# One decoder layer on one core: steps and rates of three mixing streams, and the order of the first products

## Chip, core and metric

The kernel runs on one core of a Trainium2 chip. It is one launch, and the metric is the device time of that launch in microseconds (us). Of the core's engines, TensorE (PE) multiplies and transposes, VectorE (DVE), ScalarE (ACT) and GpSimd (POOL) do the rest, and SyncE (SP) issues most transfers. Each engine works through its own queue in order.

## What is computed

One layer of a decoder: a gated feed-forward network, a mixer of two parts side by side, and a second feed-forward network, each between root-mean-square norms. It is applied to 1,024 prompt tokens and to 8 x 8 tokens of running sequences. All is float32.

```python
x = x + 0.5 * rms_norm(swiglu(rms_norm(x, norm_ffn1_pre), ffn1_w_gu, ffn1_w_down), norm_ffn1_post)
z = rms_norm(x, norm_mix_pre) @ w_in + b_in            # q, k, v, hq, hf, hi, hg
a = rms_norm(window_attention(q, k, v, sinks), attn_out_norm)          # 8 heads of 64, window 128
f = lb + (1 - lb) * sigmoid(hf)
o, S = hgrn2(silu(hq), 1 - f, log(f), hi, s0)                          # 4 heads, state 128 x 128
o = rms_norm(o, hg_out_norm) * silu(hg)
x = x + rms_norm(concat([a, o]) @ w_out, norm_mix_post)
x = x + 0.5 * rms_norm(swiglu(rms_norm(x, norm_ffn2_pre), ffn2_w_gu, ffn2_w_down), norm_ffn2_post)
```

`swiglu(x, w_gu, w_down)` is `(silu(x @ g) * (x @ u)) @ w_down` with g and u the two halves of `w_gu`; the model width is 1,024, the inner width 2,816.

## The kernel before, in words

**Tiling.** The 1,088 tokens form three groups: group 0 has 320 (256 of the prompt and the 64 sample tokens), groups 1 and 2 have 384 each (`WIDTH`, line 26). A float32 product is made of three passes (`mm3`, lines 277 to 281): both factors are split into a rounded high part and the remainder, and high by high, high by low and low by high are added in PSUM. `split` (line 257) makes the two parts, the rounding on ACT (line 258), the subtraction on DVE (line 259). Weights come in tiles of 128 x 1024 (512 KB) through three `raw` buffers, and `Ahead` (line 74) requests and splits two or three of them ahead. PSUM has eight banks, four named `mm` for the wide products and four named `ax` for everything else.

**Streams.** Work that is not a wide product is written as generators, and each `yield` ends a step. `stream(name, gen, rate)` (line 97) starts one. Each `tick()` (line 100) adds the rate to the stream's credit, and a step is traced for every whole credit. `need(name)` (line 110) traces all that is left. Ticks stand between the wide products: in a unit of `up0` (line 684) after every half of a weight tile, that is, after 12 products. So the order of a trace is wide products with steps of the streams between them; a scheduler that simulates the program then lays out each engine's queue from it.

**Mixing.** `mixer(n)` (line 1506) alternates, step by step, a recurrent side (`intra`, line 1230, then `hgrn_block` for every 128 tokens, line 1324) and an attention side (`attn_block`, line 1161); for n = 0 the samples' parts are appended to each. When one side has ended, the other gets all steps. In `intra`, each of seven levels h = 64 ... 1 multiplies parts of K (line 1299) by a decay on POOL, over all blocks at once. Then `hgrn_block` transposes K (kT, line 1335). `attn_block` computes scores (sc, line 1178), exponentials (line 1195), transposes (pT, line 1206) and products with v (pv, line 1219). `finish_attn` (line 1144) and `finish_hgrn` (line 1306) normalise 128 rows, yield once, and transpose them (oT, line 1154; hT, line 1318). The rates of the three mixers are `RM = [0.95, 1.0, 1.3]` (line 1560). Mixer 0 runs under the last products of the first feed-forward network and `w_in_units(1)`, mixer 1 under `w_out_units(0)`, `w_in_units(2)` and five units of the second network's head, mixer 2 under `w_out_units(1)` and nine such units. Other streams run beside them: c0, c1 and c2 (norms between the parts; `pre_s`, line 477, has the large splits of lines 499 and 501).

**Head.** `load_x(0, True)` (line 548) requests x of group 0 in six parts, the first halves of the columns on SP's queue and the second halves on ACT's; then two whole weight tiles follow on SP's. `pre_first` (line 556) begins with 23 products of ones that nobody reads (`warm`, line 564), transposes the gain row, and takes the sums of squares, three on ACT (line 577) and three on DVE (line 578). For each of the eight column blocks d it transposes x (line 598), after d = 1 come seven more products of ones, rounds the two parts of h (lines 605, 606), keeps x (line 607), and multiplies block d - 1 by both weight tiles of the first unit. The norm's factor is not in h yet: its row sum is broadcast by one product (rb, line 619) and multiplied in behind the products, in `both0` (line 697), for the first four units. `scaled` (line 630) makes the scaled h for all later units.

Of the kernel before, what the change touches and what calls it, by code (L numbers as in the profile page):

```python
# [8 lines left out]
F32 = mybir.dt.float32  # L9
# [5 lines left out]
ALU = mybir.AluOpType  # L15
# [24 lines left out]
NRAW = 3  # L40
WARM = 23, 7
P1 = 1.4
# [3 lines left out]
def tile_step(ctx: ExitStack, tc: tile.TileContext, A: dict, O: list):  # L46
# [10 lines left out]
    def uid(s):  # L57
        cnt[0] += 1
        return f"{s}_{cnt[0]}"

    def mmbank():
        return ps.tile([P, 512], F32, tag="mm", bufs=4, name=uid("mm"))

# [74 lines left out]
    def first_gain():  # L138
        rows = cp.tile([KC, P], F32, name="rows1")
        nc.sync.dma_start(rows, A["norm_ffn1_pre"].rearrange("o (c p) -> (o c) p", p=P))  # L140
        return rows
# [405 lines left out]

    def load_x(n, two=False):
        y = [big(F32, (P, 3, 512)), big(F32, (P, 3, 512))]
        for i in range(3):  # L550
            for hf in range(2):
                (nc.scalar if two and hf else nc.sync).dma_start(
                    y[hf][:rows_of(n, i), i], x_rows(n, i)[:, hf * 512:hf * 512 + 512])
        return y

    def pre_first(y, rows, gpre, h, raws, wts, part):

        w = WIDTH[0]  # L560
        sm = small()
        spare = axbank()

        def warm(n):
            for _ in range(n):
                last = PE.matmul(spare[:, :P], ones, ones, start=True, stop=True).ins
            return last

        last_tr = warm(WARM[0])
        V.memset(sm[:, 0, :], 1.0)  # L570
        junk2 = tmp2("junk")
        gt = axbank("gt")
        PE.transpose(gt[:, :KC], rows, ident[:KC, :KC])
        V.tensor_copy(gpre, gt[:, :KC])
        for i in range(3):
            r = rows_of(0, i)
            S.activation(junk[:r], y[0][:r, i], AF.Square, scale=D ** -0.5, accum_out=sm[:r, 0, i:i + 1])
            V.scalar_tensor_tensor(junk2[:r], y[1][:r, i], 1.0 / D, y[1][:r, i], op0=ALU.mult, op1=ALU.mult,
                                   accum_out=sm[:r, 0, 4 + i:5 + i])
        tiles = []  # L580
        for raw in raws:
            hi, lo = [pp.tile([P, KC, P], F32R, tag="wsp", bufs=8, name=uid("w")) for _ in range(2)]
            for ks in (slice(0, 4), slice(4, 8)):
                split(hi[:, ks], lo[:, ks], raw[:, ks])
            tiles.append((hi, lo))
        banks = [mmbank(), mmbank()]
        hx, x = new_h(1), [big(), big()]

        def products(d):
            for wt, bank in zip(tiles, banks):  # L590
                mm3(bank[:, :w], (wt[0][:, d, :], wt[1][:, d, :]), hcol(hx, d, w), d == 0, d == KC - 1)

        for d in range(KC):
            bank = axbank("tr")
            with tc.issue_after(last_tr):
                for i in range(3):
                    r = rows_of(0, i)
                    tr = PE.transpose(bank[:, i * P:i * P + r], y[d // 4][:r, i, (d % 4) * P:(d % 4) * P + P],
                                      ident[:r, :r])
                last_tr = tr.ins  # L600
                if d == 1:
                    last_tr = warm(WARM[1])
            hi, lo = hcol(hx, d, w)
            g = gpre[:, d:d + 1]
            last_hi = S.activation(hi, bank[:, :w], AF.Copy, scale=g)
            V.scalar_tensor_tensor(lo, bank[:, :w], g, hi.bitcast(F32), op0=ALU.mult, op1=ALU.subtract)
            (V.tensor_copy if d % 2 else S.copy)(x[d // 4][:, d % 4, :w], bank[:, :w])
            if d:
                products(d - 1)
            if d == 2:  # L610
                V.scalar_tensor_tensor(sm[:, 0, 0:3], sm[:, 0, 0:3], EPS, sm[:, 0, 4:7], op0=ALU.add, op1=ALU.add)
                rsqrt(sm[:, 1, 0:3], sm[:, 0, 0:3], (sm[:, 2, 0:3], sm[:, 3, 0:3]))
                dg = tmp2("dg")
                for i in range(3):
                    r = rows_of(0, i)
                    V.tensor_scalar(dg[:, i * P:i * P + r], ident[:, :r], sm[:, 1, i:i + 1], None, op0=ALU.mult)
            if d == 4:
                bank = axbank("rb")
                PE.matmul(bank[:, :w], ones, dg[:, :w], start=True, stop=True)
                rb = tmp2("rb")[:, :w]  # L620
                S.copy(rb, bank[:, :w])
            if d == 1:
                with tc.issue_after(last_hi.ins):
                    wts.fill()
        products(KC - 1)
# [10 lines left out]
        return (hx, rb), banks, scaled  # L636

# [11 lines left out]
    def make_ffn(wgu, wdn, h, tag):  # L649
# [33 lines left out]

        def up0(j, wts, act=None):

            w = WIDTH[0]
            g, u = mmbank(), mmbank()
            for bank in (g, u):
# [354 lines left out]
    def mixing(tp, h):  # L1043
# [100 lines left out]
        def finish_attn(n, o, r, sl):  # L1144
# [85 lines left out]
        def intra(n, res):  # L1230
# [37 lines left out]
            for h in reversed(LEVELS):  # L1268
# [11 lines left out]
                else:  # L1280
                    per = 3 if h == 32 else 2
                    for b0 in range(0, NPB[n], per):
# [8 lines left out]
                        for c in range(0, P, 2 * h):  # L1291
# [6 lines left out]
                                op=ALU.mult)  # L1298
                G.tensor_tensor(Kv[:, :, :, :h], Kv[:, :, :, :h], Dv[:, :, :, 1:2].to_broadcast([P, 4, nx, h]),
                                op=ALU.mult)  # L1300
                if h == 4:
# [4 lines left out]
        def finish_hgrn(n, bank, r, c0):  # L1306
# [6 lines left out]
            rsqrt(sm[:r, 1, :4], sm[:r, 0, :4], (sm[:r, 2, :4], sm[:r, 3, :4]))  # L1313
            V.tensor_tensor(o[:r], b4[:r], sm[:r, 1, :4].unsqueeze(2).to_broadcast([r, 4, P]), op=ALU.mult)
            yield
            tb = axbank("hT").rearrange("p (a t) -> p a t", a=4)
# [242 lines left out]

    RM = [0.95, 1.0, 1.3]  # L1560
    RA0, RA1, RB0, RB1 = 1.2, 0.75, 0.6, 0.8
# [9 lines left out]
    rows1 = first_gain()  # L1571
    xs = [load_x(0, True)]
    h = {}
    f1 = make_ffn(A["ffn1_w_gu"][0], A["ffn1_w_down"][0], h, 1)
    w0 = f1.loads0(first[1:])
    part = {}
    act, unit0, scaled = pre_first(xs[0], rows1, f1pre, h, [f1.raw0(c) for c in (first[0] * P, DFF + first[0] * P)], w0, part)
    f1.gated0(first[0], unit0, act[1])
    scaled(range(0, 2))
# [185 lines left out]
```

## Time and profile before

| | |
|---|---|
| median of 3 runs | 1997.62 us (1997.28 to 1998.98) |
| the profiled execution's own time | 1997.85 us |
| its span in the profile | 1996.1 us |
| mean granted TensorE clock | 0.995 |
| DMA | 370.28 MB, 185 GB/s |

The span is the time from the first to the last instruction of one execution. In rows of the timeline the first number is the start in us from the span's start, the second the duration in us of all the instructions in the row, then engine, line, operation, what is written and read, and how many; a bracket holds the engine's idle time just before and what ended it. In rows by stretches each engine has its busy us and its instructions, in the order PE, PEld (loading the stationary operand), DVE, ACT, POOL, then the granted TensorE clock (1.00 is full), the DMA engines' share and GB/s. TensorE's busy time includes the pipelined ends of its products, so rows overlap.

### The profile page before, as it was taken

What the parts mean: (1) busy time and instruction counts of PE and PEld (TensorE: products, weight loads), DVE (VectorE), ACT (ScalarE), POOL (GpSimd) and SP (SyncE); (2) the same over time, 40 slices, a digit from 0 to 9 for tenths busy, and PEclk for the clock granted to TensorE, in tenths of its full rate; (3) what the DMA queues carried; (4) which work ended last, traced back from release to release, by engine and by line L of the source; (5) the groups of instructions that cost most, each with busy time, mean ns of one, the idle gap of its engine ahead of it and who ended that gap; (6) DMA issues with size and microseconds to landing.
All of it is one profiled execution on the core that took longest, in us unless ns stands there. A gap on an engine that the chain in (4) does not pass through costs nothing.

```text
span 1996.1 us, 34286 instructions
## 1 busy us (share of the span) xinstructions
PE 1977.9 (99%) x13331; PEld 1859.0 (93%) x13331; DVE 1405.0 (70%) x2522; ACT 942.3 (47%) x1713; POOL 153.1 (8%) x142
## 2 busy tenths in 40 slices
PE   9999999999999999999999999999999999999998
PEld 9999999999998988779999998989999999999886
DVE  7686767886568656777668656746887887655667
ACT  5753334444445434435344543756544444444452
POOL 0000000000003102210211202000000000000201
PEclk9999999999999999999999999989999999999999
DMA  7735545655777647766334342536565555667874
GB/s 233 221 107 185 189 161 188 227 189 192 234 231 218 183 145 247 233 176 183 108 102 133 95 155 86 171 130 200 165 201 199 191 187 190 211 232 234 287 262 139
DMA packets 377316, 370.28 MB, mean 185 GB/s; under 512 B 40546, under 2 KB 294321, under 8 KB 377137
## 3 DMA queue, kind: packets, MB, share of 16 engines
q1 hardware_dynamic: 371169, 357.21, 56.3%
q10 hardware_dynamic: 5984, 10.88, 1.6%
q8 instruction: 104, 1.70, 0.3%
q14 instruction: 59, 0.48, 0.1%
HBM read 284.31 MB, written 84.71 MB: 185 GB/s over the span
## 4 chain that ended last, share of the span: by engine, by line
PE 96%; DMA 1%; ACT 1%; DVE 1%; issue 0%; POOL 0%; SPq 0%; DVEq 0%; ACTq 0%; POOLq 0%
PE mm L279 28%; PE mm L280 28%; PE mm L281 28%; PE pv L1219 1%; PE sc L1178 1%; PE c L281 1%; PE c L279 1%; PE c L280 1%; DMA raw<-in_ffn_w_gu_dram 1%; PE pT L1206 1%; PE lv L1258 1%; PE tr L511 1%; PE av L1341 0%; PE u L1348 0%; PE av L1344 0%
## 5 line engine op out<-in xcount | busy, mean ns | idle before, releaser
L279 PE MATMUL mm<-h,wsph 128*128 128x320 f32 (+1 forms) x1280 | 406.4, 319 | 0.4 <-ACT sg L676 0.4
L280 PE MATMUL mm<-h,wsph 128*128 128x320 f32 (+1 forms) x1280 | 406.1, 318 | 0.0
L281 PE MATMUL mm<-h,wspl 128*128 128x320 f32 (+1 forms) x1280 | 403.3, 317 | 0.0
L259 DVE TENSOR_TENSOR wspl<-raw,wsph 128x1024 fp32r<-128x1024 f32 x200 | 247.9, 1240 | 151.5 <-ACT wsph L258 145.9
L258 ACT CAST wsph<-raw 128x1024 fp32r<-128x1024 f32 x200 | 209.3, 1048 | 299.1 <-PE mm L280 238.4
L258 ACT CAST w<-raw 128x512 fp32r<-128x512 f32 (+1 forms) x218 | 160.3, 740 | 213.7 <-PE mm L280 113.4
L279 PEld LDWEIGHTS mm<-h,wsph 128*128 128x128 f32 x1280 | 240.7, 188 | 5.5 <-issue 3.8
L259 DVE TENSOR_TENSOR w<-raw,w 128x512 fp32r<-128x512 f32 (+1 forms) x218 | 186.6, 860 | 84.0 <-ACT w L258 83.6
L280 PEld LDWEIGHTS mm<-h,wsph 128*128 128x128 f32 x1280 | 241.0, 188 | 3.1 <-issue 2.7
L281 PEld LDWEIGHTS mm<-h,wspl 128*128 128x128 f32 x1280 | 240.3, 188 | 1.5 <-issue 1.2
L279 PE MATMUL mm<-h,w 128*128 128x384 f32 (+1 forms) x720 | 240.3, 335 | 0.5 <-ACT w L258 0.5
L280 PE MATMUL mm<-h,w 128*128 128x384 f32 (+1 forms) x720 | 240.8, 335 | 0.0
L281 PE MATMUL mm<-h,w 128*128 128x384 f32 (+1 forms) x720 | 235.4, 334 | 0.0
L280 PE MATMUL mm<-w,h 128*128 128x512 f32 x462 | 181.9, 394 | 0.0
L281 PE MATMUL mm<-w,h 128*128 128x512 f32 x462 | 180.3, 392 | 0.0
L279 PE MATMUL mm<-w,h 128*128 128x512 f32 x462 | 180.1, 393 | 0.0
L279 PE MATMUL mm<-big,w 128*128 128x384 f32 x528 | 176.4, 334 | 0.7 <-ACT big L770 0.7
L280 PE MATMUL mm<-big,w 128*128 128x384 f32 x528 | 176.5, 334 | 0.0
L281 PE MATMUL mm<-big,w 128*128 128x384 f32 x528 | 176.2, 334 | 0.0
L279 PEld LDWEIGHTS mm<-h,w 128*128 128x128 f32 x720 | 135.0, 188 | 1.1 <-ACT w L258 0.7
L280 PEld LDWEIGHTS mm<-h,w 128*128 128x128 f32 x720 | 135.2, 188 | 0.1
L281 PEld LDWEIGHTS mm<-h,w 128*128 128x128 f32 x720 | 134.7, 188 | 0.1
(355 smaller groups left out, 3531.3 us busy)
## 6 DMA issues: line engine op xcount, KB each, us to landing
raw<-in_ffn_w_gu_dram SPq DMA_DIRECT2D x156, 512.0 KB
raw<-in_ffn_w_down_dram SPq DMA_DIRECT2D x74, 512.0 KB
raw<-in_w_in_dram SPq DMA_DIRECT2D x54, 512.0 KB
ar<-fa SPq DMA_DIRECT2D x70, 384.0 KB
big<-in_ffn_w_down_dram SPq DMA_DIRECT2D x88, 256.0 KB
fb<-big SPq DMA_DIRECT2D x44, 512.0 KB
fa<-big SPq DMA_DIRECT2D x22, 768.0 KB
raw<-fb SPq DMA_DIRECT2D x30, 512.0 KB
```

Source lines behind the costliest of these rows:

```text
L258: S.copy(hi, src)
L259: (lo_eng or V).tensor_tensor(lo, src, hi.bitcast(F32), op=ALU.subtract)
L279: PE.matmul(out, a[0], b[0], start=first, stop=False, skip_group_check=resume)
L280: PE.matmul(out, a[0], b[1], start=False, stop=False, skip_group_check=resume)
L281: return PE.matmul(out, a[1], b[0], start=False, stop=last, skip_group_check=resume).ins
L511: PE.transpose(bank[:, i * P:(i + 1) * P], y[kh][:, i, k * P:(k + 1) * P], ident)
L1178: PE.matmul(banks[g][:, i * 256:i * 256 + wk], zq[64 * g:64 * g + 64, 2 * pr + i, b * P:(b + 1) * P], kx[64 * g:64 * g + 64, k0:k0 + wk], ...
L1206: PE.transpose(bank[:, (i * nk + kb) * P:(i * nk + kb + 1) * P], pt[g][:, i, kb * P:(kb + 1) * P], ident)
L1219: PE.matmul(ob[:, hd * 64:hd * 64 + 64], pT[g][:, (i * nk + kb) * P:(i * nk + kb + 1) * P], vn[:, vb, g * 64:g * 64 + 64], start=kb == 0, ...
L1258: PE.matmul(b5[32 * i:32 * i + 32, b, a], K[:, a, cs], Q[:, a, cs], start=True, stop=True)
```

## The change

Streams: one more `yield` ahead of the transposes in `finish_attn` and `finish_hgrn`; other rates; POOL's multiplication at level 64 in two instructions, the first block apart.

```diff
@@ finish_attn
             V.tensor_scalar(o[:r], o[:r], sm[:r, 1, 0:1], None, op0=ALU.mult)
+            yield
             yield
             b4 = axbank("oT").rearrange("p (c t) -> p c t", c=4)
@@ intra
-                G.tensor_tensor(Kv[:, :, :, :h], Kv[:, :, :, :h], Dv[:, :, :, 1:2].to_broadcast([P, 4, nx, h]),
-                                op=ALU.mult)
+                for xs in [slice(0, 1), slice(1, nx)] if h == 64 else [slice(0, nx)]:
+                    G.tensor_tensor(Kv[:, :, xs, :h], Kv[:, :, xs, :h],
+                                    Dv[:, :, xs, 1:2].to_broadcast([P, 4, xs.stop - xs.start, h]), op=ALU.mult)
@@ finish_hgrn
             V.tensor_tensor(o[:r], b4[:r], sm[:r, 1, :4].unsqueeze(2).to_broadcast([r, 4, P]), op=ALU.mult)
+            yield
             yield
             tb = axbank("hT").rearrange("p (a t) -> p a t", a=4)
@@
-    RM = [0.95, 1.0, 1.3]
+    RM = [0.85, 0.95, 1.2]
```

Head: twelve products of ones instead of 23 and seven; x and half weight tiles requested in one function, into buffers of the pool `big`, with the half tiles of both weights ahead of x's second column half; all squares on ACT; transposes, roundings and products in an order written out by hand, in which each engine's instruction is issued after the one named before it on that engine; the second unit's products inside the same function; the third unit's sums in `ax` banks.

```diff
-WARM = 23, 7
+WARM = 12
+    def load_first(rows, ws):
+        y = [big(F32, (P, 3, 512)), big(F32, (P, 3, 512))]
+        raws = [big(F32, (P, KC, P)), big(F32, (P, KC, P))]
+        def x_part(q, hf, i):
+            q.dma_start(y[hf][:rows_of(0, i), i], x_rows(0, i)[:, hf * 512:hf * 512 + 512])
+        nc.sync.dma_start(rows, A["norm_ffn1_pre"].rearrange("o (c p) -> (o c) p", p=P))
+        x_part(nc.sync, 0, 0)
+        x_part(nc.scalar, 0, 1)
+        x_part(nc.sync, 0, 2)
+        nc.scalar.dma_start(raws[0][:, 0:4], ws[0][:, 0:4])
+        nc.sync.dma_start(raws[1][:, 0:4], ws[1][:, 0:4])
+        for i in range(3):
+            x_part(nc.sync, 1, i)
+        for raw, w in zip(raws, ws):
+            nc.sync.dma_start(raw[:, 4:8], w[:, 4:8])
+        return [y], raws
@@ pre_first
+        def order(e, made):
+            last[e] = made.ins
+            return made
+        def after(e):
+            return tc.issue_after(last[e]) if e in last else nullcontext()
+        def squares(hf):
+            for i in range(3):
+                r = rows_of(0, i)
+                order("S", S.activation(junk[:r], y[hf][:r, i], AF.Square, scale=D ** -0.5,
+                                        accum_out=sm[:r, 0, 4 * hf + i:4 * hf + i + 1]))
+        def half(n, ks):
+            raw, (hi, lo) = raws[n], tiles[n]
+            with after("S"):
+                order("S", S.copy(hi[:, ks], raw[:, ks]))
+            with after("V"):
+                order("V", V.tensor_tensor(lo[:, ks], raw[:, ks], hi[:, ks].bitcast(F32), op=ALU.subtract))
...
+        for d in range(4):
+            turned(d)
+        squares(0)
+        half(0, lo4)
+        rounded(0)
+        rounded(1)
+        products(0, range(2))
+        half(1, lo4)
+        rounded(2)
+        rounded(3)
+        products(0, range(2, 4))
+        for d in range(4):
+            kept(d)
+        turned(4)
+        turned(5)
+        products(1, range(4))
+        for d in (4, 5):
+            rounded(d)
+        half(0, hi4)
+        turned(6)
+        turned(7)
+        half(1, hi4)
+        for d in (6, 7):
+            rounded(d)
+        products(0, range(4, 8))
+        products(1, range(4, 8))
+        with after("S"), after("V"):
+            wts.fill(1)
+        for d in range(4, 8):
+            kept(d)
+        with after("S"):
+            squares(1)
+        with after("S"), after("V"):
+            wts.fill(2)
+        V.tensor_tensor(sm[:, 0, 0:3], sm[:, 0, 0:3], sm[:, 0, 4:7], op=ALU.add)
...
+        rb = tmp2("rb")[:, :w]
+        second = [mmbank(), mmbank()]
+        for n, bank in enumerate(second):
+            wt = wts.next()
+            for d in range(KC):
+                with after("PE"):
+                    if n and d == 4:
+                        rbank = axbank("rb")
+                        order("PE", PE.matmul(rbank[:, :w], ones, dg[:, :w], start=True, stop=True))
+                        S.copy(rb, rbank[:, :w])
+                    last["PE"] = mm3(bank[:, :w], (wt[0][:, d, :], wt[1][:, d, :]), hcol(hx, d, w), d == 0, d == KC - 1)
...
-        f1.up0(first[1], w0, act)
         scaled(range(2, 5))
-        f1.up0(first[2], w0, act)
+        f1.up0(first[2], w0, act, axbank)
```

`turned(d)` is the transposes of column block d, `rounded(d)` its two parts of h (high on ACT, low on DVE), `kept(d)` the copy of x, and `products(n, ds)` the products of blocks ds with weight tile n, each with the duties it had before.

More of the change, by code (lines that the diff above doesn't have):

```diff
@@ L567, in warm @@
             return last
[L569 to L574, printed above, removed]
+        tiles = [[pp.tile([P, KC, P], F32R, tag="wsp", bufs=8, name=uid("w")) for _ in range(2)] for _ in raws]
+        banks = [mmbank(), mmbank()]
+        hx, x = new_h(1), [big(), big()]
+        last, held = {"PE": warm(WARM)}, {}
+        def order(e, made):
+            last[e] = made.ins
+            return made
@@ new lines, in half, with products @@
+        def half(n, ks):
[4 more added lines that the diff above has]
+                order("V", V.tensor_tensor(lo[:, ks], raw[:, ks], hi[:, ks].bitcast(F32), op=ALU.subtract))
+        def products(n, ds):
+            for d in ds:
+                with after("PE"):
+                    last["PE"] = mm3(banks[n][:, :w], (tiles[n][0][:, d, :], tiles[n][1][:, d, :]), hcol(hx, d, w),
+                                     d == 0, d == KC - 1)
@@ new lines, in kept @@
+        def kept(d):
+            out = x[d // 4][:, d % 4, :w]
+            if d % 2:
+                with after("V"):
+                    order("V", V.tensor_copy(out, held[d][:, :w]))
+            else:
+                with after("S"):
+                    order("S", S.copy(out, held[d][:, :w]))
+        lo4, hi4 = slice(0, 4), slice(4, 8)
+        for d in range(4):
[5 more added lines that the diff above has]
+        products(0, range(2))
@@ L587, in pre_first @@
[L587 to L624, printed above, removed]
```

58 lines of the change are left out of this document (36 added, 22 removed).

## The prediction

> **What bounds the kernel now.** The page came first, then the sums of who waited for whom on TensorE, then stretches of five microseconds wherever the granted clock was below one, then the timeline around the longest waits and of the head.
>
> ```profile
> span 1996.1 us, 34286 instructions
> PE 1977.9 (99%) x13331; PEld 1859.0 (93%) x13331; DVE 1405.0 (70%) x2522; ACT 942.3 (47%) x1713; POOL 153.1 (8%) x142
> ```
>
> TensorE is busy 99% of 1996.1 us. The diff neither adds nor removes a product, so the time can change only where TensorE stands still, or runs at a lower clock, or does work that computes nothing. These are its waits of 0.6 us and more behind the head (columns: us in total, times, longest):
>
> ```profile
> PE pT L1206 <- ACT t L1195: 2.9, 1, 2.9
> PE kT L1335 <- POOL big L1299: 2.4, 1, 2.4
> PE hT L1318 <- DVE t L1314: 0.9, 1, 0.9
> PE tr L468 <- DVE h L473: 0.9, 1, 0.9
> PE mm L279 <- ACT big L770: 0.7, 1, 0.7
> PE skT L1379 <- DMA kv<-in_cache_k_win_dram: 0.6, 1, 0.6
> ```
>
> Some 8.4 us, small. But the clock makes two of them dearer. The column after POOL is the granted clock:
>
> ```profile
> 1230.00:1235.00 5.00, 5.00 (x29) 5.00 (x28) 2.20 (x11) 4.50 (x12) 0.00 (x0) 0.66 0.00 0
> 1295.00:1300.00 5.00, 2.10 (x12) 1.40 (x10) 1.94 (x5) 4.28 (x10) 0.00 (x0) 0.86 0.54 140
> 1300.00:1305.00 5.00, 5.00 (x19) 3.67 (x17) 1.10 (x2) 4.27 (x9) 0.00 (x0) 0.50 0.19 73
> 1305.00:1310.00 5.00, 5.00 (x16) 3.85 (x16) 1.56 (x8) 0.36 (x1) 0.00 (x0) 0.50 0.10 35
> 1310.00:1315.00 5.00, 5.00 (x32) 4.91 (x31) 1.39 (x6) 2.75 (x10) 0.00 (x0) 0.77 0.00 0
> ```
>
> After the 2.4 us wait the clock is short by 0.34 x 5 = 1.7 us. After the 2.9 us wait it is short by 0.14 x 5 + 0.50 x 5 + 0.50 x 5 + 0.23 x 5 = 6.85 us, because what follows there are transposes and narrow attention products, and the clock comes back only in the last of these rows, when the wide products are under way again. The third mixer thus loses 2.4 + 1.7, 0.9 and 2.9 + 6.85: 14.75 us, nearly all that the middle of the kernel has to give.
>
> [...]
>
> **The change part by part: POOL's split (kT).** The rows of the 2.4 us wait:
>
> ```profile
> 1227.41 2.19 POOL L1299 TENSOR_TENSOR big<-big,big 128x768 f32<-128x768 f32 x1 [3.05 <-PE l L1289]
> ...
> 1229.65 0.66 PE L1335 MATMUL kT<-ident,big 128*128 128x128 f32 x4 [2.39 <-POOL big L1299]
> ...
> 1230.34 0.59 ACT L1337 COPY t<-kT 128x512 f32<-128x512 f32 x1 [2.66 <-PE kT L1335]
> ...
> 1233.20 0.61 PE L279 MATMUL mm<-h,wsph 128*128 128x320 f32 x1
> ```
>
> TensorE finishes the 64-level products at 1227.26 (1229.65 less 2.39), POOL scales K in one pass of 2.19 us over three blocks, and kT of block 0 waits for all of it. ScalarE sits in order behind kT's copy, so the banks of the dense products are not emptied either. Split, the first block is one third, 0.73 us; kT starts 1.46 us earlier and the wait is 0.93 us. The wait of 0.9 us at hT, near 1249, left no stretch below a clock of one, so the 1.7 us of clock go too: 3.2 us. The extra POOL instruction lies behind the first slice, on an engine busy 8%, and the next reader of blocks 1 and 2 is a hgrn block later. Bounds: no gain, if the half clock has come from the mixture of work, to 4.1 us.
>
> **The added steps (hT, oT).** The wait of 0.94 us is this:
>
> ```profile
> 1248.20 0.69 DVE L1314 TENSOR_TENSOR t<-av,sm 128x512 f32<-128x512 f32 x1
> ```
>
> The normalisation ends just as its transposes come up. One more yield is about two more ticks, each twelve products, at 0.147 us (13.72, 13.87, 14.01 below) 1.76 us. It covers 0.94 us: minus 0.9. What it costs is one 128 x 512 buffer of eight held for one step more; the PSUM bank is already free by then. Bounds 0 to 0.9.
>
> **The rates (pT).** The rows of the 2.9 us wait (start, duration, engine):
>
> ```profile
> 1287.34 1.22 PE L1178 MATMUL sc<-kx,big 64*128 64x256 f32 x8
> ...
> 1288.31 1.46 ACT L499 CAST h<-big 128x1536 fp32r<-128x1536 f32 x1
> ...
> 1291.92 1.75 DVE L501 TENSOR_TENSOR h<-big,h 128x1536 fp32r<-128x1536 f32 x1
> ...
> 1294.20 0.16 DVE L1189 SCALAR_TENSOR_TENSOR sm<-sm,sinkb 128x4 f32<-128x4 f32 x1
> ...
> 1295.69 1.04 ACT L258 CAST wsph<-raw 128x1024 fp32r<-128x1024 f32 x1 [2.47 <-PE mm L280]
> ...
> 1296.75 1.28 ACT L1195 ACT_TABLE_LOAD   x1
> ...
> 1298.70 2.17 PE L1206 MATMUL pT<-ident,t 128*128 128x128 f32 x8 [2.90 <-ACT t L1195]
> ```
>
> Between scores and exponentials DVE does a 1.75 us subtraction of another stream, c1 (pre_s, line 501); the small maximum row at 1294.20 sits behind it, and then the exponentials sit behind a weight cast and a table load. I count the steps in the code. mixer(2) has 52 steps, its end included; with 3 more at each side 58. Its ticks until need("m2") are 16 in w_out_units(1) and 9 x 4 in the head units: 52. Before, it needs 52 / 1.3 = 40 of them, after, 58 / 1.2 = 48.3. The recurrent side runs out after 40 steps before (tick 31) and 46 after (tick 38), and from then the attention steps stand closest together; that is the place of this wait. The stream c1 has 19 steps at 0.8, so it takes ticks 16 to 40. Before, the tail of the attention (ticks 31 to 40) lies on c1's two large splits; after (38 to 48), almost wholly behind them. Taking 1.75 us off DVE and 1.46 us off ScalarE covers 2.9 us. I take the whole wait and its clock: 9.7 us. Bounds: 0 if the weight cast and the table load alone hold it, 9.75.
>
> All three mixers must end in time: mixer(0) has 74 steps, at 0.85 that is 87 ticks of 24 + 12 + 12 + 44 = 92; mixer(1) 57 at 0.95, 60 of 80. They fit, with 5, 20 and 3.7 ticks left.
>
> **New waits.** Every queue's order is laid out anew. The nearest rows are the two waits in the first mixer's stretch, 0.94 and 0.62 us (tr, skT), and none in the second's. I charge two stages with as much again: plus 3.1 us. Bounds: 0, and 9.75 for one wait like pT.
>
> **The head.** Before, in stretches of 2 us (the first x is TensorE's passes, the last column GB/s), then in order of time:
>
> ```profile
> 0.00:2.00 2.00, 0.88 (x4) 0.88 (x5) 0.46 (x4) 1.20 (x1) 1.20 (x8) 1.00 0.01 2
> 2.00:4.00 2.00, 2.00 (x11) 2.00 (x11) 0.00 (x0) 0.39 (x2) 0.30 (x1) 1.00 0.76 263
> 4.00:6.00 2.00, 2.00 (x16) 2.00 (x15) 0.70 (x2) 0.72 (x2) 0.00 (x0) 1.00 0.99 322
> ```
>
> ```profile
> 1.12 7.23 PE L566 MATMUL ax<-ones 128*128 128x128 f32 x46 [1.12 <-DVE sm L570]
> ...
> 5.27 0.63 ACT L577 ACTIVATE junk<-big 128x512 bf16<-128x512 f32 x1 [2.86 <-DMA big<-in_x_prompt_dram]
> ...
> 10.16 1.14 ACT L258 CAST w<-raw 128x512 fp32r<-128x512 f32 x2 [0.75 <-DMA raw<-in_ffn_w_gu_dram]
> ...
> 10.81 0.69 DVE L259 TENSOR_TENSOR w<-raw,w 128x512 fp32r<-128x512 f32 x1 [0.21 <-ACT w L258]
> ...
> 11.20 0.94 ACT L605 ACTIVATE h<-tr,f1pre 128x320 fp32r<-128x320 f32 x2
> ...
> 12.16 1.00 DVE L606 SCALAR_TENSOR_TENSOR h<-tr,f1pre,h 128x320 fp32r<-128x320 f32 x2
> ...
> 12.95 0.58 PE L598 MATMUL tr<-ident,big 128*128 128x128 f32 x3
> ...
> 13.47 0.42 PE L280 MATMUL mm<-h,w 128*128 128x320 f32 x1
> ...
> 13.72 0.31 PE L281 MATMUL mm<-h,w 128*128 128x320 f32 x1
> ...
> 13.87 0.31 PE L280 MATMUL mm<-h,w 128*128 128x320 f32 x1
> ...
> 14.01 0.31 PE L279 MATMUL mm<-h,w 128*128 128x320 f32 x1
> ```
>
> From 13.47 the products run on without a wait. Four transpose groups (0.52 each, 12.95 to 13.47) and two products are done by then, 2.4 us of useful work, so it is as if it had begun at 11.1. After: x's first half and the half weight tiles are 640 and 512 KB, 1.18 MB; 0.53 MB have come by 4.0 (263 GB/s over two), the rest at 322 GB/s by 6.0, and as the two queues interleave I take 7 for the last of them. ScalarE, in its fixed order: three squares from 5.3 at 0.72 each (0.63 and its accumulator), with the short block's landing about 7.4; half cast 0.57, two roundings 0.47 each, half cast, two roundings: 10.4. DVE follows each with 0.68 or 0.50 and ends the fourth rounding at 11.4. TensorE has transposed by 8 and follows the roundings; after 11.55 it does two transpose groups (1.05), 12 products (1.76), two groups, and 24 products, bar 0.1: about 19. Of these 19 us 8 x 0.52 + 48 x 0.147 = 11.2 are useful: begun at 7.8, 3.3 us earlier. The later half of x, now wholly on SP's queue behind a weight half, lands about 9, needed at 11.55; the upper weight halves by 11, needed at 13.2. The second half's squares, moved from DVE to ScalarE, stand behind the second unit's first weight cast, 2.2 us ahead of a weight that is needed at 22.5. The third unit's sums go to attention banks, which are free, because the first two hold all four others until the row sum is there.
>
> What is late next is DVE:
>
> ```profile
> 28.00:44.00 16.00, 16.00 (x111) 16.00 (x111) 15.41 (x28) 9.41 (x17) 0.00 (x0) 1.00 0.63 186
> ```
>
> While it gated the first units and scaled the second normalisation it was busy 15.41 of 16 us, and TensorE just did not wait. After, the row sum's product stands 36 products behind 19, at about 24.3, where it stood among the transposes, and the same work is due 3.3 us earlier. I take off 1.0: minus 2.3. Bounds: minus 3.3 and plus 2 (the four transpose groups, 2.1 us, at half clock).
>
> A dozen dummy products instead of 23 (46 passes at 1.12) are 24 passes; by the rows of 4, 11 and 16 passes they end at 5.1, just as the pace has doubled. [...]
>
> **The sum.** -3.2 - 0.9 - 9.7 + 3.1 - 2.3 = -13.0 us, from the profiled execution's 1997.85 (span 1996.1 and 1.75 around it): 1984.85. That execution stands 0.23 above the median of 1997.62: 1984.6.
>
> **The rivals.** (a) The pT wait stays, or one of its kind comes back elsewhere: 1984.6 + 9.7 = 1994.3 at most, 1992 with a shorter half clock. For: weight cast and table load stay ahead of the exponentials. Against: the other five pT pairs of the third mixer did not wait. (b) The head gains nothing: a cold clock doubles 2.1 us of transposes and what lies ahead of 11.5, and the fixed order lets one late transfer stop three engines; with +2 instead of -2.3 it is 1988.9. For: it is a row of dependencies with ScalarE in each. Against: TensorE waits there anyway. (c) The streams only shuffle their waits: all of 14.75 lost again, 1997.62 - 2.3 = 1995.3, within 0.2%. That is also the case that the yields do not do what they should, if the order in the queues is not the program's. (d) Slower: the rates are too low. If my count of ticks is off by over 3.7 for mixer(2) and 5 for mixer(0), need() empties the rest with no dense product between. Scores to exponentials without cover is 1287.34 to 1298.70, 11.4 us, of which 7 to 9 bare with the clock halved behind, some 15 us, and once more in mixer(0), where wide products follow sooner, 10: 1984.6 - 3.1 + 25 = 2006.5.
>
> **How the numbers follow.** A measurement of this kernel tells about 0.2% (4 us) from no change. Forecast 0.48 (1978 to 1990), (a) 0.20, (b) 0.11, (c) 0.12, (d) 0.09. Faster by over 0.2%, below 1993.6: 0.48 + 0.11 + three quarters of (a), 0.74 + 0.04 for the better end of (c): 0.78. Within: the rest of (a) and (c), 0.13. Slower: (d), 0.09. Range: the low end takes the head's 3.3 and 3 us fewer new waits, 1980.6, and the waits of the first mixer (1.6) and the gate's whole 0.9 at kT: 1978; the high end takes in (a), (b) and most of (c): 1997.
>
> **What would show it.** POOL's line in two forms at the last level, kT's wait below 1 us; no pT wait and clock 1.00 from 1230 to 1315; no hT wait; first product at about 8.5 and 48 of them done by 19. Wrong, if a stretch at clock 0.50 appears in any mixer, if need() leaves scores and exponentials side by side, or if TensorE waits between 20 and 50 for DVE.

## The result, and the profile after

| | before | after |
|---|---|---|
| median of 4 executions each | 1998.30 us (1997.28 to 1999.31) | 1975.05 us (1974.46 to 1979.19) |
| ratio, 95% interval | | 0.9888 (0.9871 to 0.9905) |
| profiled execution | 1997.85 us, span 1996.1 | 1975.32 us, span 1973.6 |

The kernel is 22.6 us faster than the 1997.62 on which the prediction was made. Forecast were 13.0, and the range ended at 1978.0, 3 us above the result. The direction was right, the size was not, and the sum of steps hides that two of them were wrong in what they stand for.

First the page's head and TensorE's waits after (us in total, times, longest; there are no others):

```profile
span 1973.6 us, 34235 instructions
PE 1960.7 (99%) x13295; PEld 1846.4 (94%) x13295; DVE 1405.5 (71%) x2517; ACT 952.5 (48%) x1724; POOL 153.7 (8%) x145
...
PE ax L278 <- ACT wsph L257: 1.7, 1, 1.7
PE av L1427 <- DVE big L1378: 1.2, 1, 1.2
PE ax L586 <- DVE sm L601: 1.1, 1, 1.1
PE mm L279 <- DVE h L1222: 1.0, 1, 1.0
PE mm L279 <- DVE h L639: 0.3, 1, 0.3
```

Behind the head only two waits are left, 1.2 + 1.0 = 2.2 us; before there were 8.9 us of them. None of before's is here: not pT, not kT, not hT, and not the four small ones either. The stretches behind kT, which now starts at 1221.83, and around the third mixer's last score products, where the clock was at half before (it is the column after POOL):

```profile
1220.00:1225.00 5.00, 3.81 (x43) 3.48 (x42) 3.32 (x3) 1.95 (x4) 1.68 (x2) 1.00 0.51 155
1225.00:1230.00 5.00, 5.00 (x39) 4.98 (x38) 3.52 (x15) 4.95 (x21) 0.00 (x0) 1.00 0.30 112
...
1295.00:1300.00 5.00, 5.00 (x37) 4.99 (x36) 1.88 (x4) 4.19 (x11) 0.00 (x0) 1.00 0.37 108
1300.00:1305.00 5.00, 5.00 (x40) 4.41 (x39) 3.58 (x10) 3.75 (x6) 0.00 (x0) 1.00 0.44 112
1305.00:1310.00 5.00, 5.00 (x38) 4.99 (x36) 2.00 (x9) 4.36 (x11) 0.00 (x0) 1.00 0.37 131
```

Full clock throughout. So far this is what the prediction asked to see, although the pT wait did not go for the reason that it gave (see the rates, below). What it did not look for shows only when TensorE's groups are set side by side, by line and shape (busy us, mean ns of one). Of before:

```profile
L1178 PE MATMUL sc<-kx,big 64*128 64x256 f32 x112 | 25.7, 421 | 0.0
```

and of after:

```profile
L1259 PE MATMUL sc<-kx,big 64*128 64x256 f32 x112 | 18.1, 402 | 0.0
```

The same 112 score products take 7.6 us less, though one of them by itself takes about as long as before. The timeline says why. Before, in the third mixer:

```profile
1238.78 1.13 PE L1178 MATMUL sc<-kx,big 64*128 64x256 f32 x4
...
1242.22 1.13 PE L1178 MATMUL sc<-kx,big 64*128 64x256 f32 x4
```

After, the same products:

```profile
1232.96 1.13 PE L1259 MATMUL sc<-kx,big 64*128 64x256 f32 x8
```

A group of eight works on two head groups, whose operands lie on the first and on the last 64 partitions. Standing next to each other in TensorE's queue, all eight take as long as four of one head group alone: 1.06 us from the first start to the next instruction's, against twice 1.06 when other work lies between. Counted over the whole trace, 7 of the 14 groups were apart before and 2 are after, so 5 x 1.06 = 5.3 us went; the rest of the 7.6 is the half clock of one group near 1305, which the clock's term counts.

The head, in order of time after:

```profile
9.00 0.42 PE L278 MATMUL mm<-h,w 128*128 128x320 f32 x1
...
15.03 3.10 SPq L707 DMA_DIRECT2D xT<-big  x2
...
19.12 0.31 PE L278 MATMUL mm<-h,wsph 128*128 128x320 f32 x1
...
27.71 1.04 ACT L257 CAST wsph<-raw 128x1024 fp32r<-128x1024 f32 x1 [5.96 <-DMA raw<-in_ffn_w_gu_dram]
...
28.81 0.41 PE L278 MATMUL ax<-h,wsph 128*128 128x320 f32 x1 [1.65 <-ACT wsph L257]
```

At 19.12 the first unit's 48 products and all transposes are done, where 19 was forecast; by the forecast's own arithmetic the useful work began at 7.9, 3.2 us earlier than before. But at 28.81 TensorE waits 1.65 us for a weight tile of the third unit, so about 1.5 us are left.

**The account in spans** (1996.1 to 1973.6, 22.5 us): pT's wait and clock 9.75; kT's 4.1, less the new 1.2 at av behind it, 2.9; hT 0.9; the small waits 2.6 less the new 1.0, 1.6; scores 5.3; head 1.5. Together 21.95; 0.55 stay unassigned.

### The profile page after: what moved, and what is told of

It reads as the page before. It is cut to its first block, busy times and chain, and to the rows that moved or that the text cites. A ratio compares the mean times of both kernels' runs of the same rounds, so it can differ in the third digit from the quotient of the medians.

```text
span 1973.6 us, 34235 instructions
## 1 busy us (share of the span) xinstructions
PE 1960.7 (99%) x13295; PEld 1846.4 (94%) x13295; DVE 1405.5 (71%) x2517; ACT 952.5 (48%) x1724; POOL 153.7 (8%) x145
## 4 chain that ended last, share of the span: by engine, by line
PE 98%; DMA 1%; DVE 1%; ACT 0%; issue 0%; SPq 0%; DVEq 0%; ACTq 0%
PE mm L278 29%; PE mm L279 29%; PE mm L280 29%; PE pv L1300 1%; PE c L278 1%; PE c L280 1%; PE c L279 1%; PE sc L1259 1%; PE lv L1339 1%; PE pT L1287 1%; PE tr L510 1%; DMA raw<-in_ffn_w_gu_dram 0%; PE su L1552 0%; PE u L1431 0%; PE av L1424 0%; PE av L1427 0%
## 5 line engine op out<-in xcount | busy, mean ns | idle before, releaser
L279 PE MATMUL mm<-h,wsph 128*128 128x320 f32 (+1 forms) x1264 | 400.5, 317 | 1.0 <-DVE h L1222 1.0
L278 PE MATMUL mm<-h,wsph 128*128 128x320 f32 (+1 forms) x1264 | 401.0, 319 | 0.0
L280 PE MATMUL mm<-h,wspl 128*128 128x320 f32 (+1 forms) x1264 | 398.5, 317 | 0.0
L279 PEld LDWEIGHTS mm<-h,wsph 128*128 128x128 f32 x1264 | 237.5, 188 | 4.9 <-issue 3.1
L278 PEld LDWEIGHTS mm<-h,wsph 128*128 128x128 f32 x1264 | 237.0, 188 | 4.0 <-issue 3.5
```

The costliest lines, as they stand in the source:

```text
L278: PE.matmul(out, a[0], b[0], start=first, stop=False, skip_group_check=resume)
L279: PE.matmul(out, a[0], b[1], start=False, stop=False, skip_group_check=resume)
L280: return PE.matmul(out, a[1], b[0], start=False, stop=last, skip_group_check=resume).ins
```

## The experiments

Each is the kernel before, or the kernel after, with one part changed; none leaves out any of the layer's work. The intervals are of the ratio to the kernel before, run on the same chip. They are about 0.35% wide (7 us), so a difference of 2 to 4 us between two versions lies within them and is believed only as far as rows of the traces show it.

**1. Streams without the head (mix_only): the kernel before with both added steps, the rates and POOL's split.**

> The kernel before with the streams' edits alone (two yields, POOL's split, new rates), head as before. By the account of the two traces the middle gives 15.2 us of waits and half clock and 5.3 us of attention scores that run two at a time, the head 1.5 us: 1998.3 - 20.5 = 1978. Rival, the head is worth more than its rows show (7 us, as what the predicted 13 us leave out): 1983.

Measured: 1978.53, ratio 0.9906 (0.9889 to 0.9922): 19.1 us, where the account in spans has 20.5 without the head.

**2. The head alone (head_only): the kernel after with the old streams.**

> The changed head with the streams as before. By the account 1998.3 - 1.5 = 1997, with the same long waits in the third mixer unless the earlier start shuffles them. Rival, the head is worth 7 us: 1991.

Measured: 1995.67, ratio 0.9991 (0.9982 to 1.0000), so about 2 us; between experiment 1 and the whole change lie 3.5. Its waits in the middle are before's (pT 2.9, kT 2.4, hT 0.9). By medians the two halves add up to 21.1 of the 22.6 us, which is the same within the intervals, and the streams are nearly all of it.

**3. The changed kernel without the added steps (no_yields).**

```diff
             V.tensor_scalar(o[:r], o[:r], sm[:r, 1, 0:1], None, op0=ALU.mult)
             yield
-            yield
```

(and the same in `finish_hgrn`).

> The changed kernel without the two added yields. If the yields are what lets the scores' two banks be free together, seven of sixteen score groups fall apart again where three did, each 1.06 us more, and the hT wait of 0.9 us comes back: 1975 + 4.2 + 0.9 = 1980. Rival, the yields cover a wait of 0.9 us and nothing else (as predicted): 1976.

Measured: 1989.14 (1984.70 to 1992.12), ratio 0.9956 (0.9940 to 0.9973). Both expectations were too low. Its longest wait, with rates and split in place:

```profile
PE oT L1234 <- DVE t L1230: 3.6, 1, 3.6
```

The pT wait is gone as the prediction wants it, but the last oT waits 3.6 us for its normalisation, and 5 groups of scores are apart against 2. With the rates one long wait went and another came.

**4. The changed kernel with the old rates (old_rates).**

```diff
-    RM = [0.85, 0.95, 1.2]
+    RM = [0.95, 1.0, 1.3]
```

> The changed kernel with the old rates. If the rates took the pT wait away (as predicted) it is back with its half clock: 1975 + 9.7 = 1985, clock 0.50 for some 13 us near 1280. Rival, any new layout would have lost it, or the yields did: 1975 to 1977.

Measured: 1977.66, ratio 0.9903 (0.9888 to 0.9918). The pT wait is 0.5 us, and the profiled execution's mean clock is 0.999, as after. In the whole change the rates are worth 2.6 us by the medians, with intervals that overlap; two groups of scores (4 apart against 2) make 2.1 of it.

**5. The kernel before with both added steps alone (yields_b).**

> The kernel before with the two added yields and nothing else. If the yields do the work of the middle: the long waits and their half clock go (up to 15.2 us) and four of the score groups that were split come together (4.2 us): 1997.65 - 19.4 = 1978, above it as far as new waits stand. If the rates or POOL's split were needed (as predicted), only the hT wait of 0.9 us goes: 1996.7.

Measured: 1983.55, ratio 0.9929 (0.9915 to 0.9944): 14.7 us, where the prediction had 0.9. Its waits behind the head:

```profile
PE kT L1337 <- POOL big L1300: 2.4, 1, 2.4
PE pT L1207 <- ACT t L1196: 1.1, 2, 0.6
...
PE spv L1419 <- DVE t L1414: 0.8, 1, 0.8
PE pv L1220 <- DVE t L1210: 0.6, 1, 0.6
```

kT is untouched, as it must be without the split, and pT is down to two waits of 0.6 at most. By spans (1996.1 to 1982.5): pT and clock 9.75 less 1.1; hT 0.9; three groups of scores (4 apart against 7) 3.2; small waits 2.6 less 1.4. That is 13.95 of 13.6 us. The pT wait is small although only 27 wide passes lie between scores and transposes, against 48 before. By the rows c1's large subtraction, which stood between these scores and their exponentials (1291.92), now ends at 1285.6, ahead of the scores at 1293.72, and the exponentials begin 5.5 us after the scores, where it was 10.7. So the added steps, with the old rates, do what the prediction expected of the rates.

**6. POOL's split left out of the change (no_split).**

```diff
-                for xs in [slice(0, 1), slice(1, nx)] if h == 64 else [slice(0, nx)]:
-                    G.tensor_tensor(Kv[:, :, xs, :h], Kv[:, :, xs, :h],
-                                    Dv[:, :, xs, 1:2].to_broadcast([P, 4, xs.stop - xs.start, h]), op=ALU.mult)
+                G.tensor_tensor(Kv[:, :, :, :h], Kv[:, :, :, :h], Dv[:, :, :, 1:2].to_broadcast([P, 4, nx, h]),
+                                op=ALU.mult)
```

> The changed kernel with POOL's multiplication at level 64 in one instruction again. As predicted, kT waits 1.5 us longer and the clock falls for one 3.4 us window: 1975 + 3.2 = 1978. Rival, the yields have moved kT away from it, and the split is worth nothing: 1975; in the trace kT then does not wait.

Measured: 1978.56, ratio 0.9908 (0.9893 to 0.9923), with the kT wait of 2.4 us back and the profiled execution's mean clock at 0.997, against 0.999 after: the split is worth 3.5 us by the medians, close to the 4.1 that the wait and its half clock took before, though the intervals overlap. With the split, in the kernel after, the rows are:

```profile
1221.11 0.62 POOL L1381 TENSOR_TENSOR big<-big,big 128x256 f32<-128x256 f32 x1 [2.11 <-PE l L1370]
1221.83 0.66 PE L1418 MATMUL kT<-ident,big 128*128 128x128 f32 x4
1221.98 1.05 POOL L1381 TENSOR_TENSOR big<-big,big 128x512 f32<-128x512 f32 x1 [0.25 <-PE l L1370]
1221.99 1.85 DVE L1378 TENSOR_TENSOR big<-big,big 128x768 f32<-128x768 f32 x1 [1.13 <-PE l L1370]
...
1223.90 0.49 PE L1427 MATMUL av<-st,big 128*128 128x128 f32 x2 [1.19 <-DVE big L1378]
```

kT waits for nothing now. What is late next is DVE's scaling of Q by the same decay, 1.85 us, still in one instruction over all blocks, and av waits 1.19 us for it. The prediction left 0.93 us at POOL; the size is right and the engine is not.

**7. Score products in a given order.** In the kernel before chained as the source has them, the head groups alternating (paired_b), and in the kernel after one head group behind the other (unpaired_a):

```diff
@@ attn_block, paired_b
+                behind = None
                 for i in range(2):
                     for g in range(2):
-                        PE.matmul(banks[g][:, i * 256:i * 256 + wk], ...
+                        with tc.issue_after(behind) if behind else nullcontext():
+                            behind = PE.matmul(banks[g][:, i * 256:i * 256 + wk], ...
@@ attn_block, unpaired_a: the same with
-                for i in range(2):
-                    for g in range(2):
+                for g in range(2):
+                    for i in range(2):
```

> The kernel before with the four score products of a group chained on TensorE, head group 0 and 1 in turn, so that none of its eight split groups can fall apart. If two products on different row halves run side by side and two on the same half do not, eight groups lose 1.06 us each, one of them twice that at half clock: 1997.65 - 8 = 1990 with the long waits left as they are. If the spacing is the same either way: 1997.7. Waits may move, the trace tells them apart.

> The changed kernel with the four score products chained the other way, both of head group 0 and then both of group 1. Paired groups of eight passes take 1.06 us, split ones 2.12; twelve of them and two narrow ones fall apart: 1975 + 12 x 1.06 + 0.9 = 1988.6. Rival, the order does not matter: 1975.

Measured: paired_b 1996.24, ratio 0.9989 (0.9979 to 0.9998). The chain only turned four and four into two and six:

```profile
1238.08 0.70 PE L1180 MATMUL sc<-kx,big 64*128 64x256 f32 x2
...
1241.39 1.13 PE L1180 MATMUL sc<-kx,big 64*128 64x256 f32 x6
```

That is 0.63 + 1.06 us instead of 2.12, 3 us over seven groups by starts, of which the median shows 2; one more wait came (skT, 1.9 us against 0.6). Here the chain fixed the order of the products and did not bring all eight together.

unpaired_a: 1977.16, ratio 0.9898 (0.9883 to 0.9913). Expected was a loss of some 13 us; it is 2, and its profiled span (1973.7) is that of the kernel after. A miss: eight products next to each other take 1.07 us in this order too.

```profile
1233.03 1.14 PE L1261 MATMUL sc<-kx,big 64*128 64x256 f32 x8
```

So the order within the eight made no difference here, and standing together did.

**8. One added step at a time, in the kernel before (oT_yield, hT_yield), and the third mixer's rate alone (rate2_b).**

```diff
-    RM = [0.95, 1.0, 1.3]
+    RM = [0.95, 1.0, 1.2]
```

> The kernel before with the one added step ahead of oT in finish_attn alone. By the prediction this step covers no wait at all: 1998, within 0.1% of before. By what both steps gave together (1983.55 against 1998.21, 14.7 us): if it is the attention side's own step that matters, because it moves every later attention step of a mixer by one, then the pT wait and its half clock behind 1298 go (9.7) and the score products, of which seven groups of eight stand apart in fours before, stand together in all but about one (its queue order has 2 rows of two score products against 16 before; some 0.9 us each, 5): 1984, and the 0.9 us wait at hT stays. If the gain came from the recurrent side: 1996 or more.

> The kernel before with the one added step ahead of hT in finish_hgrn alone. By the prediction: the 0.94 us wait at hT goes and nothing else, 1997.1. The rival, that any shift of the alternation by a step moves the third mixer's attention off the stream c1: the pT wait and its half clock go here too, 1987 or less, with three of the seven split groups of score products together again (10 rows of two in the queue order against 16).

> The kernel before with the third mixer's rate alone at 1.2 instead of 1.3: the step to which the prediction gave 9.7 us. By the prediction the tail of the attention comes to lie behind c1, no pT wait, clock 1.00 behind 1290: 1988.5. By the runs since (with the old rates and both added steps the pT wait was only 0.5): the rate does little by itself, the wait moves or stays, and the time is 1994 to 2000; the number of split score groups stays at seven.

Measured: oT_yield 1992.93 (1989.10 to 1995.63), ratio 0.9970 (0.9958 to 0.9982); hT_yield 1992.66, ratio 0.9972 (0.9960 to 0.9983); rate2_b 1994.84, ratio 0.9986 (0.9977 to 0.9996). Neither step alone is the 14.7 us. In waits, oT_yield:

```profile
PE pT L1207 <- ACT t L1196: 2.6, 1, 2.6
PE kT L1336 <- POOL big L1300: 2.4, 1, 2.4
PE oT L1155 <- DVE t L1150: 2.4, 2, 1.5
```

hT_yield's longest:

```profile
PE oT L1154 <- DVE t L1150: 3.6, 1, 3.6
```

rate2_b, its waits and its clock:

```profile
PE oT L1154 <- DVE t L1150: 3.6, 1, 3.6
...
1320.00:1325.00 5.00, 1.50 (x7) 1.53 (x8) 2.70 (x10) 1.20 (x5) 0.00 (x0) 0.70 0.36 130
1325.00:1330.00 5.00, 5.00 (x24) 5.00 (x23) 1.89 (x4) 3.06 (x6) 0.00 (x0) 0.61 0.20 67
```

The lower rate alone does just what the prediction's step says: c1's subtraction now starts at 1285.25, ahead of the scores at 1293.95, and there is no pT wait. And the end of the attention, later now and as bare as before, waits 3.6 us at oT (near 1323) instead, and loses (0.30 + 0.39) x 5 = 3.45 us of clock behind it. With the step ahead of hT alone the outcome is of the same kind: 3.6 us at oT, and between 1315 and 1330 (0.35 + 0.50 + 0.17) x 5 = 5.1 us of clock. With the step ahead of oT alone there is a pT wait again, but at the next scores: those of 1306.18, with no wide product between them and their transposes.

**9. The same number of steps behind the transposes (late_yields), and two steps ahead instead of one (two_yields), in the kernel before.**

```diff
@@ late_yields, finish_attn and finish_hgrn
             put_mix(n, 0, sl, m[:, :, :r])
             yield
+            yield
@@ two_yields, finish_attn and finish_hgrn, ahead of the transposes
             yield
+            yield
+            yield
```

> The kernel before with the same two additional steps, but put behind the transposes and the stores of their result, at the end of finish_attn and finish_hgrn, so that every stream has exactly as many steps as with the steps ahead (1983.55), and nothing stands between a normalisation and its transposes. If the gain comes from the distance between normalisation and transposes, the waits oT and hT stay (0.9 to 3.6 each, with half clock): 1992 or more. If it comes from the longer streams alone, that is from another alternation and a shorter tail in which attention stands alone: the pT wait goes all the same, about 1984 to 1986.

> The kernel before with two additional steps ahead of the transposes instead of one. If more steps ahead are cover, the waits on the normalisations stay away as with one step: 1983 to 1986 (kT's wait of 2.4 stays). If the one step only happened upon an order without a long wait, any other order has waits of 2 to 4 us again in the third mixer, with half clock behind them, as each single step had: 1989 to 1996.

Measured: late_yields 2000.52, ratio 1.0007 (0.9998 to 1.0016); two_yields 1984.46, ratio 0.9925 (0.9909 to 0.9942). With the streams as long, but nothing more between normalisation and transposes, there is no gain:

```profile
PE pT L1207 <- ACT t L1196: 4.4, 1, 4.4
PE hT L1319 <- DVE t L1315: 4.0, 3, 2.9
```

With one more step of distance, and another order, the gain is the same 14 us, and of the third mixer's waits only kT is left. The first one is new, in the first mixer's samples:

```profile
PE sav L1467 <- POOL t L1455: 2.9, 1, 2.9
PE kT L1339 <- POOL big L1301: 2.4, 1, 2.4
```

So the place of the added step counts, and not the number of steps. The distance that it makes explains the waits at oT and hT. It does not by itself explain those at pT: the 4.4 us of late_yields belong to scores at 1251.74, another pair than before's, whose exponentials begin 10.2 us later. Which pair is left bare, and by what, depends on the order, and no run holds the order fixed. Over all kernels that were run one thing holds without exception: the eight with a step ahead of both oT and hT have no wait over 1.2 us in the third mixer, bar kT where POOL's split is left out; the eight that lack one or both have one of 2.6 to 4.4 us there, at pT or at oT.

**10. The head's late weight tile (xt_a): the stores of xT moved from SP's queue to ACT's.**

```diff
-        for hf in range(2):
-            nc.sync.dma_start(xT[:, 4 * hf:4 * hf + 4, :w], x[hf][:, :, :w])
+        with after("S"):
+            for hf in range(2):
+                nc.scalar.dma_start(xT[:, 4 * hf:4 * hf + 4, :w], x[hf][:, :, :w])
```

> The changed kernel with the two stores of xT moved from SP's queue to ACT's, behind the last ordered instruction of ScalarE in the head. If the third unit's weight tile comes late (27.7) because SP's queue stands behind those stores, which wait for DVE's last copies of x, then it is requested some 3 us earlier and the wait of 1.7 us at ax goes, without a new one: 1973.5, span 1972. If the tile is late because the 16 DMA engines are full with the upper halves of x, the weights and the caches, the wait stays at 1 to 2 us: 1975. If ScalarE, which now issues the stores, is held up by them, the wait stays and others come: 1977.

Measured: 1973.87 (1973.69 to 1974.26), ratio 0.9878 (0.9861 to 0.9894), the fastest of all. The wait is gone (the other six kernels with this head have 0.5 to 1.9 us of it), but not for the reason expected:

```profile
18.80 9.93 SPq L264 DMA_DIRECT2D raw<-in_ffn_w_gu_dram  x4
19.27 1.85 ACTq L708 DMA_DIRECT2D xT<-big  x2
...
26.03 1.05 ACT L257 CAST wsph<-raw 128x1024 fp32r<-128x1024 f32 x1 [3.76 <-DMA raw<-in_ffn_w_gu_dram]
```

The tile is requested at 18.80, not earlier than after's (18.68, behind the stores that SP issued from 15.03), because its buffer comes free no sooner: DVE's subtraction of an earlier tile ends at 18.78 here and at 18.66 in after. It lands 1.7 us earlier, for the cast that waits for it begins at 26.03 instead of 27.71: the 1.28 MB of stores now start behind the request instead of ahead of it. By these rows the transfers were late, not the queue. One profile of each carries little weight, though: three of the six others wait only 0.5 to 0.6 us, with the stores where the change has them. The intervals of this version and of the change overlap; the wait that went is 1.65 us in the profiles, the medians differ by 1.2.

## Why the prediction came out as it did

**POOL's split: right.** 3.2 forecast, 3.5 by leaving it out, 2.9 by the trace's account. The kT wait did cost its clock as well (1.7 us before), and without the wait the clock held (1.00 from 1220 to 1230 after). That cost is not certain in every execution: in the profiles of oT_yield and two_yields the same 2.4 us at kT left the clock at 1.00.

**The added steps: the step that failed.** The prediction gave them 0.9 us, the one wait at hT that the trace showed, and said that their cost is a buffer held for a step longer. They are 14.7 us alone, and 14.1 are lost without them. What the runs show in place of the 0.9: they keep covered whatever normalisation stands at the end of a bare piece of attention, wherever the order puts it (3.6 us at oT in no_yields, rate2_b and hT_yield; behind it the clock is short by 3.45 us in rate2_b and 5.1 in hT_yield, and in no_yields the four transposes oT take 1.09 us, where four of them take 0.60 after); they change the order, so that in yields_b c1's subtraction no longer delays the exponentials; and three groups of scores come together. The trace of before shows only the one hT wait because in that particular order the pT wait comes first; rate2_b shows what comes behind it. Why both steps together avoid a long pT wait in every order that was run stays open.

**The rates: wrong in their worth, and in the whole change in their mechanism too.** The tail of the attention was to lie almost wholly behind c1's two large splits, which would take 1.75 us off DVE. In rate2_b and no_yields the subtraction does come ahead of the scores whose transposes waited before. In the kernel after it does not:

```profile
1288.03 1.13 PE L1259 MATMUL sc<-kx,big 64*128 64x256 f32 x4
...
1292.44 1.76 DVE L500 TENSOR_TENSOR h<-big,h 128x1536 fp32r<-128x1536 f32 x1
...
1296.15 0.51 ACT L1276 ACTIVATE t<-t,sm 128x256 f32<-128x256 f32 x1
...
1299.98 0.38 PE L1287 MATMUL pT<-ident,t 128*128 128x128 f32 x2
```

The subtraction (L500, which is L501 before) still stands between the scores and their exponentials. By the rows two other things took the wait away: of the two weight casts that stood between scores and exponentials on ScalarE one now comes behind (1298.23), so that the exponentials begin 8.1 us after the scores instead of 10.7, and 63 wide passes lie between scores and transposes instead of 48, 9.3 us of cover instead of 7.3. That this stage came out without a wait, as forecast, was partly luck.

The worth failed as well. A lower rate alone does take the pT wait away, but the prediction then stopped: it asked at POOL what is late next, and not here, where it booked 9.7 us. Alone the third mixer's rate brings 3.3 us, in the whole change all three bring 2.6. Of rival (a), "one of its kind comes back elsewhere", three runs that lack the step ahead of oT are examples: no_yields, rate2_b and hT_yield, with 3.6 us at oT. The long half clock behind pT was put down to transposes and narrow attention products; of the ten microseconds from 1300 to 1310 transposes take only about 1.4, score products and products with v nearly all the rest, and what kept the clock down so long is not shown.

**New waits: 3.1 us charged, none due.** Two stages were to have as many waits as the first mixer; the whole middle has 2.2 us instead of 8.9, and outside the third mixer's terms the small waits fell by 1.6. With the charge that is 4.7 us of the miss.

**Scores: a term left out.** 5.3 us. The row of eight score products at 1287.34 was quoted, and the rows of four were in the same timeline; that both take about 1.2 us was not read. The prediction had ruled such a term out at its start, where time could change only by waits, by the clock or by products that compute nothing: the same products took less time because of their neighbours. It is the other half of the miss of some 10 us: 13.0 + 5.3 + 4.7 is 23.0 of 22.5, head and kT giving 1.1 back and 0.55 unassigned.

**The head: right in its start, wrong in what is late next.** First product 9.00 (8.5 forecast), 48 products by 19.12 (19), and a worth of 2.0 to 3.5 us around the 2.3 forecast. Not DVE took some of it back but a weight tile; a dozen products of ones ran until 6.6, not 5.1, all 24 passes at the slow pace of 0.23 us (5.49 us in all; the fourteen passes at 9.58 before took 0.12 each), without harm: the four groups of transposes behind them took 2.29 us (6.71 to 9.00), 0.57 each as the two at 8.44 before. Of the 2 us that the upper bound and rival (b) gave to transposes at half clock this trace shows nothing.

**Rates too low, rival (d): did not occur.** Scores and exponentials have products between them in all three mixers: no wait at pT is left.

## What to carry to other kernels

A long wait in a trace marks the first place where a chain is bare, not the only one: before a cure is booked at the full wait, follow the chain to its next hand-over and ask whether that one has cover. Where work is interleaved by steps, put the step between the producer and its reader on another engine; as many steps elsewhere in the stream bought nothing here (2000.52 us against 1998.47). When a wait has gone, look whether the cause that you named has gone with it: here it was still there. And when only the order changes, compare the same instructions' time group by group: here two sets of products on different partitions cost half when they stood together (1.06 us against 2.12), and no wait shows it.

## Unexpected in the hardware

**Half clock came in multiples of one length, and not every time.** In the kernel before the two stretches, cut to their ends:

```profile
1230.45:1233.86 3.41, 3.41 (x18) 3.41 (x18) 1.71 (x8) 3.38 (x10) 0.00 (x0) 0.51 0.00 0
1298.60:1312.25 13.65, 13.55 (x47) 10.55 (x48) 3.75 (x14) 7.86 (x21) 0.00 (x0) 0.50 0.17 52
```

3.41 us, and 13.65, four times as much. The clock lost behind oT above, 3.45 us in rate2_b and 5.1 in hT_yield, is 6.9 and 10.2 us at half clock: by this estimate about two and three times 3.41. Whether a wait of 2.4 or 2.6 us costs any clock varied: in oT_yield both are there, at 1227 and 1309, and the profiled execution kept full clock behind them:

```profile
1225.00:1230.00 5.00, 2.56 (x24) 2.55 (x24) 2.08 (x5) 2.25 (x8) 2.24 (x1) 1.00 0.45 136
1230.00:1235.00 5.00, 5.00 (x38) 5.00 (x37) 4.45 (x19) 4.43 (x17) 0.00 (x0) 1.00 0.06 21
1305.00:1310.00 5.00, 2.41 (x21) 1.90 (x20) 3.09 (x12) 1.51 (x5) 0.00 (x0) 1.00 0.38 126
1310.00:1315.00 5.00, 4.89 (x38) 4.41 (x38) 2.23 (x5) 4.49 (x11) 0.00 (x0) 1.00 0.00 0
```

Its six executions go from 1989.10 us (mean clock 0.999) to 1995.63 (0.995). Why the same wait costs clock at one time and not at another is not shown. The kernel xt_a, without a wait over 1.2 us, stays within 0.6 us in four executions.
